# Loading the first piece of A through GpSimd's casting DMA queue, beside the first piece of B on SyncE's queue

## The chip, the cores and the metric

The kernel runs on one core of one Trainium2 chip. The metric is the device time of one execution in microseconds (us). Beside it stands a profile of one execution, whose span runs from the first instruction to the last. Engines are named as the profile names them: PE is TensorE's matmul, PEld its weight load, DVE is VectorE, ACT is ScalarE, POOL is GpSimd, SP is SyncE. SPq is SyncE's sequencer, which issues DMAs.

## What is computed

A product of two 2048x2048 fp32 matrices, then layer normalisation along each row of the product, with gamma and beta along the row.

```python
def reference(a, b, gamma, beta, eps):
    x = np.matmul(a, b)
    mean = np.mean(x, axis=-1, keepdims=True)
    var = np.var(x, axis=-1, keepdims=True)
    normalized = (x - mean) / np.sqrt(var + eps)
    return (gamma * normalized + beta).astype(np.float32)
```

## The kernel before

The product is made in fp16 with fp32 accumulation. A is cut into 16 row tiles of 128 rows, B into 16 blocks of 128 rows of the contraction (called kt), and the 2048 columns of the product into four PSUM banks of 512. B is kept whole in SBUF as fp16 (`b16`), after a cast on the chip. TensorE needs A transposed, with the contraction on the partitions; the transposed tiles are called `at`.

The row tiles fall in two kinds. Tiles 0 to 3 (the head) are worked on while B still arrives, so that a block of B that has landed is used at once for four row tiles. For this A's first 512 rows come in 16 pieces of 128 rows by 512 columns (256 KB), and B in 32 half blocks of 128 rows by 1024 columns (512 KB). Tiles 4 to 15 come later, by other helpers, with all of B in place: TensorE then only runs matmuls, one bank of 16 after the other.

A piece of the head goes through four steps, each a helper:

- `load_first(n)` (line 94): SyncE issues a DMA from HBM to an fp32 buffer `f` (pool `firstp`, 4 buffers).
- `cast_first(n)` (line 99): VectorE casts it to fp16, buffer `h` (pool `first16`, 2 buffers).
- `turn_first(n)` (line 105): TensorE transposes it in four 128x128 blocks into a PSUM bank, with `ident`, a unit matrix that GpSimd finishes on line 304.
- `keep_first(n)` (line 109): VectorE copies the bank to `at`.

A half block of B goes through `load_b` (line 76, SyncE's queue) and `cast_left` or `cast_right`, where VectorE casts 512 columns (lines 81, 86) and ScalarE the other 512 (lines 82, 87).

The order of the instructions on each engine is written out by hand: within a `manual_schedule` block every engine runs its instructions in program order. In the head the order of the DMAs on SyncE is piece 0 of A, half block 0 of B, piece 1, half block 1, and so on up to piece 3 and half block 3; the right halves follow. Loads carry one of eight completion counters in turn, so that the ninth DMA of the queue waits until the first has landed, the tenth until the second, and so on.

TensorE begins with ten matmuls on a buffer of zeros (`warm_up(10)`, line 302), whose result nobody uses; three or two more such matmuls stand in further places of the head. After the first ten comes `turn_first(0)`. Then a loop over n from 0 to 3 issues, for VectorE: `keep_first(n)`, the cast of half block n of B, `cast_first(n + 1)`; for ScalarE the other half of the cast of B; for TensorE some matmuls that are ready, the transposes of piece n + 1, and the rest of the matmuls. After the loop the four row tiles' left columns for kt 0 to 3 are completed and put by in SBUF (`put_by`, lines 150 and 152), and the right columns follow.

GpSimd has little to do in the head. Besides `ident` it issues the loads of row tiles 6 to 15 (line 115), much later, all of them plain fp32.

Of the kernel before, what the change touches and what calls it, by code (L numbers as in the profile page):

```python
# [10 lines left out]
FP16 = mybir.dt.float16  # L11
# [4 lines left out]
def kernel(  # L16
# [18 lines left out]
    nc = tc.nc  # L35
    P = 128
# [13 lines left out]
    first16 = ctx.enter_context(tc.tile_pool(name="first16", bufs=2))  # L50
# [21 lines left out]
    a_in, b_in, t_of, tile_in, part = {}, {}, {}, {}, {}  # L72

    def load_b(kt, h, queue=None):
        w = bigp.tile([P, NH], FP32, tag="big", name=f"w{kt}_{h}")
        (queue or nc.sync).dma_start(w, b_rows[kt // 4, kt % 4][:, ds(h * NH, NH)])
        b_in[kt, h] = w
# [9 lines left out]
        nc.scalar.copy(b16[:, kt, NH + NB:N], w[:, NB:NH])  # L87

    pieces = [(g, c) for c in range(4) for g in range(G)]

    def load_first(n):
        g, c = pieces[n]
        f = firstp.tile([P, 4 * P], FP32, tag="first", name=f"f{g}_{c}")
        nc.sync.dma_start(f, a[ts(g, P), ts(c, 4 * P)])
        a_in[n] = f

    def cast_first(n):
        h = first16.tile([P, P, 4], FP16, tag="h", name=f"h{n}")
        nc.vector.tensor_copy(h.rearrange("m p t -> m (p t)"), a_in[n])
        a_in[n] = h  # L100

    def turn_first(n):
        t_of[n] = psum.tile([P, 4, P], FP16, tag="c_ps", bufs=8, name=f"t_ps{n}")
        for t in range(4):
            nc.tensor.transpose(t_of[n][:, t, :], a_in[n][:, :, t], ident)
# [188 lines left out]
    with tc.manual_schedule(engines=order):  # L294
# [5 lines left out]
        def warm_up(n):  # L300
            for _ in range(n):
                nc.tensor.matmul(w_ps, warm[:, 0:P], warm, start=True, stop=True)  # L302

        nc.gpsimd.affine_select(
            out=ident, in_=ident, compare_op=AluOp.not_equal, fill=1.0,
            base=0, pattern=[[-1, P]], channel_multiplier=1,
        )
        K1 = 4
        for t in range(K1):
            load_first(t)  # L310
            load_b(t, 0)
        for t in range(K1):
            load_b(t, 1)
# [23 lines left out]


        warm_up(10)
        cast_first(0)  # L340
        turn_first(0)
        warm_up(3)
        for n in range(K1):
# [187 lines left out]
```

## Time and profile before

| | |
|---|---|
| time, median of 3 runs | 246.25 us (245.3, 246.28, 246.25) |
| the profiled execution | 244.86 us, with a span of 243.1 us |
| PE busy | 231.8 us, 95% of the span |
| DVE busy | 198.3 us, 82% |
| ACT busy | 92.9 us, 38% |
| POOL busy | 89.0 us, 37% |
| granted TensorE clock, mean | 0.994 |

When the first loads are issued and when they have landed, from the profile's list of DMA issues and its list of instructions in order of time; the landing is the issue's start plus the time to landing:

| load | name in the profile | issue | to landing | landed |
|---|---|---|---|---|
| piece 0 of A, 256 KB | f_0_106 | 0.74 | 4.4 | 5.1 |
| half block 0 of B, 512 KB | w_0_108 | 1.17 | 5.2 | 6.4 |
| piece 1 | f_0_110 | 1.64 | 5.6 | 7.2 |
| half block 1 | w_0_112 | 2.11 | 6.5 | 8.6 |
| piece 2 | f_0_114 | 2.58 | 6.7 | 9.3 |
| half block 2 | w_0_116 | 3.06 | 7.5 | 10.6 |
| piece 3 | f_0_118 | 3.71 | 7.5 | 11.2 |
| half block 3 | w_0_120 | 4.34 | 8.1 | 12.4 |

In the profile a row of the list in order of time gives the start and the length in us, the engine, the line, the operation, what it writes and reads, how many instructions are merged, and in brackets how long the engine had been idle before it and what ended that idle time. Starts are counted from the start of the span.

### The profile page before, as it was taken

Reading aid. Unit: us, or ns where it says so; the run is one execution under the profiler, and the core shown is the slowest. Engines: PE = TensorE matmul, PEld = TensorE weight load, DVE = VectorE, ACT = ScalarE, POOL = GpSimd, SP = SyncE. Lnnn points to the kernel's source line nnn. Section 1 sums busy time; section 2 is a strip of 40 time slices with the busy share of each in tenths; the row PEclk is TensorE's granted clock in tenths of the full one; section 3 lists DMA queues with packets and bytes.
Section 4 is the critical chain, followed back from the end, with each engine's and each line's share of the span. In section 5 each row is a group of like instructions: output and inputs, shape, how many; then the busy total and the mean of one; then the engine's idle time right before and its main releaser. Section 6 shows DMA issues by size and latency. Waiting matters only on the chain.

```text
span 243.1 us, 3398 instructions
## 1 busy us (share of the span) xinstructions
PE 231.8 (95%) x1139; PEld 108.2 (45%) x1139; DVE 198.3 (82%) x373; ACT 92.9 (38%) x165; POOL 89.0 (37%) x168
## 2 busy tenths in 40 slices
PE   7999899999999999999999999999999999999960
PEld 2445455444444444444444444444444444446440
DVE  1577764894399999998999899998999895966962
ACT  2373524453314330461908255370917391020020
POOL 0000000000786498897966807693760000000011
PEclk9999999999999999999999999999999999999997
DMA  4999999998699859584775626483684222030405
GB/s 163 403 402 389 369 390 412 408 409 212 187 206 302 216 164 287 180 281 124 262 204 208 229 97 235 154 291 89 215 211 175 96 86 89 32 141 0 175 0 173
DMA packets 22129, 52.66 MB, mean 217 GB/s; under 512 B 4448, under 2 KB 9056, under 8 KB 21856
## 3 DMA queue, kind: packets, MB, share of 16 engines
q1 hardware_dynamic: 16704, 41.74, 46.8%
q0 software_dynamic: 5120, 10.50, 17.3%
q10 hardware_dynamic: 288, 0.21, 0.3%
q8 instruction: 9, 0.15, 0.2%
q14 instruction: 8, 0.07, 0.1%
HBM read 35.65 MB, written 16.78 MB: 216 GB/s over the span
## 4 chain that ended last, share of the span: by engine, by line
PE 91%; DMA 3%; DVE 3%; SPq 1%; ACT 0%; issue 0%; DVEq 0%
DMA f_0_114<-in_a_dram 3%; PE ps_last_2349 L226 1%; PE ps_3_2245 L137 1%; PE ps_0_2190 L137 1%; PE ps_1_2086 L137 1%; PE ps_2_1998 L137 1%; PE ps_3_1904 L137 1%; PE ps_0_1839 L137 1%; PE ps_1_1740 L137 1%; PE ps_2_1644 L137 1%; PE ps_3_1544 L137 1%; PE ps_0_1479 L137 1%; PE ps_1_1386 L137 1%; PE ps_2_1284 L137 1%; PE ps_2_1169 L137 1%; PE ps_3_1072 L137 1%
## 5 line engine op out<-in xcount | busy, mean ns | idle before, releaser
L211 ACT ACTIVATE junk<-b_93 128x1024 f16<-128x1024 f16 x32 | 33.7, 1054 | 0.5
L115 POOL DMA_DIRECT2D p_0_240<-in_a_dram x8 | 4.5, 570 | 60.6 <-DMA p_1_211<-in_a_dram 60.6
L265 POOL TENSOR_TENSOR u_last_n<-u_last_n,gamma_b 128x128 f32<-128x128 f32 x1 | 0.5, 453 | 53.8 <-ACT u_last_n L264 53.8
L226 PEld LDWEIGHTS <-at_2062 128*128 128x128 f16 x96 | 8.8, 98 | 5.4
L137 PEld LDWEIGHTS <-at_420 128*128 128x128 f16 x64 | 6.0, 98 | 8.5 <-DVE b_93 L81 1.0
L137 PEld LDWEIGHTS <-at_1000 128*128 128x128 f16 x64 | 6.3, 98 | 7.5
L137 PEld LDWEIGHTS <-at_1240 128*128 128x128 f16 x64 | 6.3, 98 | 7.5
L137 PEld LDWEIGHTS <-at_959 128*128 128x128 f16 x64 | 6.3, 98 | 7.5
L137 PEld LDWEIGHTS <-at_1362 128*128 128x128 f16 x64 | 6.3, 98 | 7.5
L137 PEld LDWEIGHTS <-at_1716 128*128 128x128 f16 x64 | 6.3, 98 | 7.5
L137 PEld LDWEIGHTS <-at_1838 128*128 128x128 f16 x64 | 6.3, 98 | 7.5
L137 PEld LDWEIGHTS <-at_1600 128*128 128x128 f16 x64 | 6.3, 98 | 7.6
L137 PEld LDWEIGHTS <-at_1127 128*128 128x128 f16 x64 | 6.3, 98 | 7.6
L137 PEld LDWEIGHTS <-at_1009 128*128 128x128 f16 x64 | 6.2, 98 | 7.6
L137 PEld LDWEIGHTS <-at_1478 128*128 128x128 f16 x64 | 6.2, 98 | 7.6
L137 PEld LDWEIGHTS <-at_1954 128*128 128x128 f16 x64 | 6.2, 98 | 7.6
L137 PEld LDWEIGHTS <-at_421 128*128 128x128 f16 x64 | 6.1, 98 | 7.4 <-DVE at_421 L109 0.6
L137 PEld LDWEIGHTS <-at_422 128*128 128x128 f16 x64 | 6.3, 98 | 6.5
L137 PEld LDWEIGHTS <-at_423 128*128 128x128 f16 x64 | 6.3, 98 | 6.4
L302 PE MATMUL w_ps<-warm 128*128 128x512 f16 x19 | 6.5, 481 | 1.2 <-DVE warm L295 1.2
L115 POOL DMA_DIRECT2D p_0_366<-in_a_dram x8 | 4.3, 550 | 8.0 <-ACT a_0_1620 L121 5.5
L115 POOL DMA_DIRECT2D p_0_402<-in_a_dram x8 | 4.3, 549 | 5.4 <-ACT a_0_1858 L121 5.4
(575 smaller groups left out, 643.2 us busy)
## 6 DMA issues: line engine op xcount, KB each, us to landing
gamma_b<-in_gamma_dram SPq DMA_DIRECT2D x1, 1024.0 KB, 7.4
beta_b<-in_beta_dram SPq DMA_DIRECT2D x1, 1024.0 KB, 11.8
w_0_108<-in_b_dram SPq DMA_DIRECT2D x1, 512.0 KB, 5.2
w_0_112<-in_b_dram SPq DMA_DIRECT2D x1, 512.0 KB, 6.5
w_0_116<-in_b_dram SPq DMA_DIRECT2D x1, 512.0 KB, 7.5
w_0_120<-in_b_dram SPq DMA_DIRECT2D x1, 512.0 KB, 8.1
w_1_122<-in_b_dram SPq DMA_DIRECT2D x1, 512.0 KB, 8.6
w_1_124<-in_b_dram SPq DMA_DIRECT2D x1, 512.0 KB, 8.7
```

The costliest lines, as they stand in the source:

```text
L115: queue.dma_start(f[ds(32 * q, 32), c], a_pieces[q, 2 * h + c][:, ds(4 * i, 4)])
L137: nc.tensor.matmul(x_of[i, q], at[i][:, kt, :], b16[:, kt, ds(q * NB, NB)], start=(kt == lo), stop=(kt == hi - 1),)
L211: nc.scalar.activation(junk, b16[:, kt, ds(h * NH, NH)], ActFn.Copy, accum_out=b_sum[:, h, kt:kt + 1])
L226: nc.tensor.matmul(x[:, 0:w], at[last][:, t, :], b16[:, t, ds(lo, w)], start=(t == 0), stop=(t == n_kt - 1))
L265: nc.gpsimd.tensor_tensor(y, y, gamma_b[:, ds(lo, w)], AluOp.mult)
L302: nc.tensor.matmul(w_ps, warm[:, 0:P], warm, start=True, stop=True)
```

## The change

Piece 0 of A no longer goes through SyncE's queue and VectorE. A new helper lets GpSimd issue one DMA that reads the same 128 rows by 512 columns as fp32 from HBM and writes them as fp16 straight to the `h` buffer. It stands ahead of GpSimd's `affine_select`, which finishes `ident`. SyncE starts with half block 0 of B. `cast_first(0)` is gone, and the transposes of piece 0 wait for the DMA instead of VectorE. The other 15 pieces are as before.

```diff
+    def load_first_cast():
+        h = first16.tile([P, P, 4], FP16, tag="h", name="h0")
+        nc.gpsimd.dma_start(h.rearrange("m p t -> m (p t)"), a[0:P, 0:4 * P])
+        a_in[0] = h
...
+        load_first_cast()
         nc.gpsimd.affine_select(
             out=ident, in_=ident, compare_op=AluOp.not_equal, fill=1.0,
             base=0, pattern=[[-1, P]], channel_multiplier=1,
         )
         K1 = 4
         for t in range(K1):
-            load_first(t)
+            if t:
+                load_first(t)
             load_b(t, 0)
...
         warm_up(10)
-        cast_first(0)
         turn_first(0)
         warm_up(3)
```

## The prediction

> **What bounds the kernel now.** I read the page first, then the chain of waits, then the head instruction by instruction.
>
> ```profile
> span 243.1 us, 3398 instructions
> PE 231.8 (95%) x1139; PEld 108.2 (45%) x1139; DVE 198.3 (82%) x373; ACT 92.9 (38%) x165; POOL 89.0 (37%) x168
> PE   7999899999999999999999999999999999999960
> PE 91%; DMA 3%; DVE 3%; SPq 1%; ACT 0%; issue 0%; DVEq 0%
> ```
>
> PE fills every slice but the first and the last; the chain that ended last is PE for 91% and DMA for 3%. So a change in the head counts only if it moves the point from which PE runs without a gap, and then it moves the end by as much. The chain in order of time tells where that point is:
>
> ```profile
> 2.58 6.66 DMA f_0_114<-in_a_dram
> 9.24 0.03 issue
> ...
> 9.34 0.44 DVE h_465 L99
> 9.78 0.05 issue
> 9.82 0.41 PE t_ps_473 L105 x4
> 10.23 0.22 PE ps_0_467 L137
> ```
>
> The chain does not start at piece 0, which this change moves, but at piece 2 (f_0_114): it lands at 9.24, is cast, and is transposed at 9.82. From there PE goes on to 14.6, and, over some copies, to the end. Piece 0 matters only if it moves these transposes. Rows of the list in order of time, for the rounds before:
>
> ```profile
> 5.18 0.43 DVE L99 CAST h_434<-f_0_106 128x512 f16<-128x512 f32 x1 [3.96 <-DMA f_0_106<-in_a_dram]
> 5.66 0.41 PE L105 MATMUL t_ps_436<-ident,h_434 128*128 128x128 f16 x4 [0.52 <-DVE h_434 L99]
> 6.11 0.42 DVE L109 COPY at_420<-t_ps_436 128x512 f16<-128x512 f16 x1 [0.51 <-PE t_ps_436 L105]
> 7.24 0.43 DVE L99 CAST h_447<-f_0_110 128x512 f16<-128x512 f32 x1 [0.36 <-DMA f_0_110<-in_a_dram]
> 9.34 0.43 DVE L99 CAST h_465<-f_0_114 128x512 f16<-128x512 f32 x1 [0.31 <-DMA f_0_114<-in_a_dram]
> ```
>
> VectorE goes round a loop: cast a piece, wait for its transposes, keep them, cast a block of B, cast the next piece. Ahead of the casts of pieces 1 and 2 it is idle for 0.36 and 0.31 us, until the DMA: loads pace the head, with 0.67 us of slack in VectorE's loop between piece 0 and piece 2. Last, what the DMAs do (the columns after the second number are busy times by engine, then clock, DMA share, GB/s):
>
> ```profile
> 2.00:4.50 2.50, 2.50 (x7) 0.91 (x6) 0.00 (x0) 0.02 (x1) 0.00 (x0) 1.00 0.55 150
> 4.50:13.50 9.00, 8.10 (x47) 3.59 (x46) 4.80 (x12) 2.47 (x4) 0.00 (x0) 1.00 1.02 399
> ```
>
> From 4.5 us the 16 DMA engines are full, at 399 GB/s. From 2.0 to 4.5 they are busy for 55%, although SyncE has issued four loads (1.5 MB) by 2.58 us. So the ramp has room, and the rest has none.
>
> **What the Trainium skill says.** "DMA: Bandwidth & Descriptors", section "Issuing engines are not separate DMA queues": DMAs of SyncE, ScalarE and GpSimd run on the same 16 engines and interleave; a second issuer saves only issue time. The trace has one queue alone in the head, at 399 GB/s, and cannot confirm it; if it holds, moving piece 0 to another queue leaves the bytes ahead of piece 2 unchanged. Same page, "Latency and other measured facts": the first byte comes after some 0.6 us on the hardware path, 1 us on GpSimd's. The trace agrees in the order, with larger numbers: SyncE's first issue is at 0.74 and 49 GB/s are seen between 1.5 and 2.0, nothing earlier; GpSimd's first load is issued at 62.20, its queue shows no bytes before 63.6 and shows some from there, 1.4 us later. "SBUF — State Buffer", section "SBUF: two separate sides": VectorE's fast copies can keep GpSimd from writing descriptors. Here VectorE only clears three small buffers, 0.86 to 1.22 us, then sleeps until 5.18, so at most some 0.4 us. "TensorE: Matmul & The Clock Gate", Part 1: an idle window of some 3.4 us halves the clock; the trace has a gap of 0.52 us here and no drop.
>
> **The change part by part.**
>
> *VectorE:* one cast of 0.43 us goes, and 0.05 us to the transposes: 0.48 us between landing and transposing. It is worth that only if the piece lands as early as before, at 5.1. The ten warm-up matmuls end at 5.14, so the first transposes can't come before that: at most 0.52 us earlier than 5.66.
>
> *SyncE:* one issue goes from the front. Half block 0 is issued at 0.74 instead of 1.17, the later ones 0.43 to 0.47 us earlier, until landings pace them. The ninth DMA, which waits for the first, is now the tenth of before (w_1_124): it waits for half block 0, as before. Nothing starts sooner on a full DMA system, since the issues run ahead of the data anyway: piece 2 is issued 6.7 us before it lands. Worth nothing by itself. In the pool of fp32 pieces, piece 4 finds an unused buffer; the others still wait for the cast of the piece four back.
>
> *GpSimd:* one DMA is added. Its issue costs 0.55 to 0.71 us, from the rows of line 115:
>
> ```profile
> 62.20 4.50 POOL L115 DMA_DIRECT2D p_0_240<-in_a_dram  x8 [60.62 <-DMA p_1_211<-in_a_dram]
> ```
>
> eight in 4.50 us, the longest 0.714. Behind it stands only the unit matrix: from 1.28 it slips to about 1.5 and ends near 1.8, long before the transposes. GpSimd's own loads follow at 62.2 and later; their counters move by one place, onto a load long landed. No cost.
>
> *The landing of piece 0.* This is the number that decides, and no casting DMA is in the trace. Issue at 0.74, first bytes 1.4 us later: 2.1 us. From below: its 64 KB loads take 2.5 us at the shortest; 192 KB more at 399 GB/s are 0.5, so 3.7 us. From above: p_0_258's loads, beside saturated engines, took 7.9 us, so 8.6 us. Between: piece 0 and half block 0 together, 768 KB, had landed by 6.4 before. If the two queues share the engines equally, piece 0 is through when 512 KB have moved, halfway between 5.1 and 6.4: 5.75; if it gets only a third, at 6.4. I take 6.0, with transposes at 6.05: 0.39 us later than before. Half block 0 lands by 6.4 either way.
>
> *Carried forward:* the 0.39 us eat into the slack of 0.67: piece 1 is cast at 7.27 instead of 7.24, piece 2 at 9.34 as before. The break-even is a landing at 5.66 + 0.67 - 0.05 = 6.28. Piece 2's own landing stays where it is, since the bytes ahead of it are the same. PE waits 0.9 us after its warm-up instead of 0.52: far below the window above.
>
> *Sum on the span:* 243.1 + 0 = 243.1. The profiled execution, 244.86, lies 1.4 us below the median of the timed ones, which themselves span 1 us; a repeated median may move within that. I put the sum on the median, 246.25 + 0, and name 246.2.
>
> **The rivals.**
>
> *A, as above: absorbed.* 246.2 us, own range 245.3 to 247.0, chance 0.52. For it: the slack, and a chain that starts at piece 2.
>
> *B, the ramp fills: faster.* Two rings let the engines use part of the 45% of 2.5 us, 1.1 us, that they idle in the ramp. Piece 0 lands by 4.7, and the stream behind runs about 0.5 us early. The transposes of piece 0 begin at 5.14, the loop could have those of piece 2 at 5.14 + (9.82 - 5.66 - 0.67) = 8.63. Half block 3 limits next: VectorE's cast of it ends at 13.42, its first user starts at 13.96, so 0.54 without an earlier landing. Together -0.5 to -1.0; I take -0.7: 245.5 us. Against it: nothing shows that the ramp's slowness belongs to the queue rather than to the engines or HBM. Chance 0.22.
>
> *C, the casting piece is late or heavy: slower.* If converting slows the engines, the piece takes more than its 0.65 us (256 KB at 399 GB/s) of all sixteen, and everything behind is pushed. At a quarter of the rate that is 2.6 us, 1.95 more ahead of piece 2; at a half 0.65 more. A late start alone does the same to the loop: each us of landing past 6.28 is a us at the end. I take a third of the rate, +1.3: 247.5 us; it decides from 6.28 on. For it: an operation that the trace does not show, at the cold start of a queue, whose loads took 7.9 us when the engines were full. Against it: those few descriptors compete with half-idle engines. Chance 0.26.
>
> **How the numbers follow.** Outside 0.5% (1.23 us, about what a measurement of this kernel can tell from no change), B lies for about half of its chance once the runs' own spread is allowed for, 0.11, and A for 0.05 on either side; C for three quarters, 0.20. Faster 0.16, same 0.59, slower 0.25. The range takes A and most of B and C: 245.0 to 247.9.
>
> **What would show it.** A: the chain still starts at piece 2 with a landing near 9.2, and transposes of piece 0 between 5.6 and 6.3. B: a DMA share well above 0.55 from 2.0 to 4.5, piece 2 landing at 8.8 or sooner. C: the first transposes after 6.3, the chain starting at GpSimd's load, or fewer GB/s from 4.5 on. I am wrong if piece 0 lands past 6.3, or if piece 2's landing moves by more than 0.3 us.

## The result and the profile after

| | before | changed |
|---|---|---|
| time, median of 4 runs | 245.78 us | 249.11 us |
| all runs | 245.11 to 246.28 | 248.94 to 249.59 |
| ratio, with 95% interval | | 1.014, 1.0106 to 1.0175 |
| span of the profiled execution | 243.1 us | 247.2 us |
| first transposes of piece 0 / 1 / 2 / 3, us from the start of the span | 5.66 / 7.79 / 9.82 / 12.23 | 8.13 / 11.05 / 13.38 / 15.76 |

The change costs 3.3 us. Some executions of any kernel fall into a slower state; medians here and below are of all executions, while the ratios leave out two such, one of run e3 and one of run e8 below. The page of the changed kernel, with the rows that answer to those of before: PE's busy share by slices of the span, the granted clock, and the chain that ended last.

```profile
span 247.2 us, 3396 instructions
PE   7699899999999999999999999999999999999960
PEclk9799999999999999999999999999999999999995
PE 81%; DMA 8%; DVE 6%; SPq 2%; issue 1%; ACT 1%; DVEq 0%; POOLq 0%
```

PE's share of the chain went from 91% to 81%, DMA's from 3% to 8%, and the clock has a dip in its second slice. Two loads make up most of the 8%: 2.8% are piece 0, at the start, and 4.0% a half block of B much later. The chain of waits in order of time (start, length, what) shows both:

```profile
1.26 6.83 DMA h_103<-in_a_dram
8.08 0.05 issue
8.13 0.43 PE t_ps_434 L110 x4
...
10.40 0.85 PE w_ps L307 x2
11.26 0.43 PE t_ps_453 L110 x4
11.68 0.85 PE w_ps L307 x2
12.54 0.36 PE ps_0_465 L142
12.89 0.22 PE ps_1_466 L142
...
13.54 0.22 PE t_ps_471 L110 x4
...
53.63 9.78 DMA w_1_200<-in_b_dram
```

The chain no longer starts at piece 2 but at GpSimd's load: issued at 1.26, landed 6.83 us later. From 10.40 on two warm-up matmuls take 0.85 us, at 12.89 one product takes 0.22: in between PE ran at half speed. The load at 53.63 has no counterpart in the chain of the kernel before; the experiments come back to such loads. The list in order of time, and the table by stretches (after the times: PE, PEld, DVE, ACT, POOL busy, clock, DMA share, GB/s), show the same from the engines' side:

```profile
1.26 0.72 POOL L93 DMA_DIRECT2D h_103<-in_a_dram  x1 [0.81 <-POOLq L518]
8.13 0.41 PE L110 MATMUL t_ps_434<-ident,h_103 128*128 128x128 f16 x4 [2.49 <-DMA h_103<-in_a_dram]
8.58 0.42 DVE L114 COPY at_420<-t_ps_434 128x512 f16<-128x512 f16 x1 [7.36 <-PE t_ps_434 L110]
```

```profile
2.00:4.50 2.50, 2.50 (x7) 0.88 (x6) 0.00 (x0) 0.24 (x2) 0.31 (x1) 1.00 0.81 246
9.50:12.50 3.00, 3.00 (x11) 1.26 (x10) 0.95 (x4) 0.66 (x2) 0.00 (x0) 0.50 1.03 418
16.00:24.00 8.00, 7.82 (x45) 3.61 (x43) 5.49 (x13) 4.22 (x8) 0.00 (x0) 1.00 0.66 242
```

PE stood for 2.49 us, and the clock granted from 9.5 to 12.5 was 0.50. VectorE stood for 7.36 us behind the transposes of piece 0, with every later cast of the head behind it in its order. The third stretch is the surprise: from 16 to 24 us the DMAs moved 242 GB/s. In the kernel before it was

```profile
16.00:24.00 8.00, 7.82 (x46) 3.70 (x45) 6.34 (x16) 4.52 (x9) 0.00 (x0) 1.00 1.03 393
```

The waits of SyncE's queue up to 30 us say why (waited in all, times, longest). The changed kernel, then the kernel before:

```profile
SPq L99 <- DVE h_548 L104: 5.9, 1, 5.9
```

```profile
SPq L94 <- DVE h_550 L99: 2.4, 1, 2.4
...
SPq L94 <- DMA f_1_126<-in_a_dram: 1.6, 1, 1.6
```

These are waits ahead of the load of piece 8, which needs the buffer that VectorE's cast of piece 4 gives free. Before, SyncE stood 4.0 us there, 1.6 until piece 4 had landed and 2.4 more until it was cast; now it stood 5.9 us for the cast alone. The load was issued at 21.69 instead of 18.16, with the half blocks of B behind it, and the DMA engines ran dry.

### The profile page after: what moved, and what is told of

The parts are those of the page before. It is cut to its first block, busy times and chain, and to the rows that moved or that the text cites. A ratio compares the mean times of both kernels' runs of the same rounds, so it can differ in the third digit from the quotient of the medians.

```text
span 247.2 us, 3396 instructions
## 1 busy us (share of the span) xinstructions
PE 233.9 (95%) x1139; PEld 108.9 (44%) x1139; DVE 197.4 (80%) x372; ACT 92.9 (38%) x165; POOL 89.9 (36%) x169
## 4 chain that ended last, share of the span: by engine, by line
PE 81%; DMA 8%; DVE 6%; SPq 2%; issue 1%; ACT 1%; DVEq 0%; POOLq 0%
DMA w_1_200<-in_b_dram 4%; DMA h_103<-in_a_dram 3%; SPq L120 2%; PE ps_0_1008 L142 1%; PE ps_last_2347 L231 1%; PE ps_3_2243 L142 1%; PE ps_0_2188 L142 1%; PE ps_1_2084 L142 1%; PE ps_2_1996 L142 1%; PE ps_3_1902 L142 1%; PE ps_0_1837 L142 1%; PE ps_1_1738 L142 1%; PE ps_2_1642 L142 1%; PE ps_3_1542 L142 1%; PE ps_0_1477 L142 1%; PE ps_1_1384 L142 1%
## 5 line engine op out<-in xcount | busy, mean ns | idle before, releaser
L307 PE MATMUL w_ps<-warm 128*128 128x512 f16 x19 | 8.0, 563 | 1.2 <-DVE warm L300 1.2
```

## The experiments

Two questions were open after this: why GpSimd's load landed at 8.1 (its queue, or the conversion on the way), and how transposes of piece 0 that came 2.5 us late became 3.3 us at the end, and 4.1 in the profiled execution.

**Queue or conversion.** Run e1 keeps the place of the load and takes the conversion away:

```diff
-        h = first16.tile([P, P, 4], FP16, tag="h", name="h0")
-        nc.gpsimd.dma_start(h.rearrange("m p t -> m (p t)"), a[0:P, 0:4 * P])
-        a_in[0] = h
+        f = firstp.tile([P, 4 * P], FP32, tag="first", name="f0_0")
+        nc.gpsimd.dma_start(f, a[0:P, 0:4 * P])
+        a_in[0] = f
...
         warm_up(10)
+        cast_first(0)
         turn_first(0)
```

> Piece 0 on GpSimd's queue as plain fp32, cast by VectorE as before; nothing is converted in flight. Theory 'queue' (GpSimd's queue starts late and then gets its turns slowly beside SyncE's loads; converting matters little): landing 6 to 7 us after its issue, near 7.4 to 8.1 in the span, first transposes 0.5 later than that, time 249.1 to 249.8 us. Theory 'conversion' (the cast in flight is what is slow): landing by 5.8, first transposes by 6.3, time 245.8 us as before.

Measured: 249.47 us, ratio to before 1.0168 (1.0135 to 1.0201). The plain load took 6.3 us to land where the casting one took 6.8, and with VectorE's cast the first transposes came at 8.10. Its row:

```profile
f<-in_a_dram POOLq DMA_DIRECT2D x1, 256.0 KB, 6.3
```

So it is the queue; the conversion accounts for no more than the half microsecond between the two landings, with one trace of each. Run e2 is e1 with `nc.scalar.dma_start`: a second hardware queue.

> Piece 0 on ScalarE's hardware queue as plain fp32, cast by VectorE as before, beside half block 0 of B on SyncE's. Theory 'queue': a second hardware queue has no late start and an equal share, so landing 5.5 to 6.4, first transposes by 6.9, time 245.8 to 246.4 us. Rival 'beside' (any second queue loses its turns to SyncE's loads): landing 7 or later, time 247 us or more.

Measured: 245.68 us, ratio 1.0008 (0.9994 to 1.0022), no difference from before. The load was issued at 0.74, where GpSimd's was at 1.28, took 5.1 us, and the first transposes came at 6.37. Piece 0 beside half block 0 on two queues is thus harmless when the second queue is ScalarE's. Run e5 leaves the changed kernel's load alone with the engines for a while, by clearing the buffer of half block 0 twice on GpSimd, so that SyncE starts at 4.30:

```diff
         w = bigp.tile([P, NH], FP32, tag="big", name=f"w{kt}_{h}")
+        if (kt, h) == (0, 0):
+            nc.gpsimd.memset(w, 0.0)
+            nc.gpsimd.memset(w, 0.0)
```

> The changed kernel with SyncE's first load held back: its buffer is cleared twice by GpSimd after the unit matrix, so SyncE issues nothing before about 4.5 us and the casting load has the DMA engines to itself until then. Theory 'busy engines' (the queue starts late because SyncE's loads fill the engines): first bytes of GpSimd's queue 1.4 us after its issue at 1.26, by 2.9 us, and landed by 4.2 us. Theory 'cold queue' (the first load on GpSimd's queue is late whatever else runs): first bytes at 4.4 to 4.6 again, then landed by 5.5 us. The time is not the point: all loads of B come over 3 us later.

Measured: the load landed 3.5 us after its issue at 1.25, and the first transposes came at 5.41. Packets of GpSimd's queue (q0; q1 is SyncE's) in the stretches from 0 to 2.7 and 2.7 to 3.7 us of this run (queue: packets, MB, share of 16 engines):

```profile
q0 software_dynamic: 3, 0.00, 0.7%
...
q0 software_dynamic: 86, 0.08, 51.7%
```

The same for the changed kernel from 0 to 4.6 and from 4.6 to 7.9 us:

```profile
q1 hardware_dynamic: 222, 0.68, 56.1%
q0 software_dynamic: 4, 0.00, 0.5%
...
q1 hardware_dynamic: 290, 0.84, 76.9%
q0 software_dynamic: 140, 0.13, 23.1%
```

With the engines to itself the queue shows its first packets some 1.4 us after the issue, as at 62 us in the kernel before; beside SyncE's loads only after 3.3 us. Then it gets 23% of the engines' time and needs 3.2 us for what takes it 1.8 alone. Of the two theories "cold queue" falls and "busy engines" holds. The run, at 248.4 us (one execution), was no slower than the changed kernel, although all loads of B came 3.6 us later.

**What a late piece 0 costs.** Run e4 exchanges the first two loads of the kernel before on SyncE's queue:

```diff
         for t in range(K1):
-            load_first(t)
+            if t:
+                load_first(t)
             load_b(t, 0)
+            if t == 0:
+                load_first(t)
```

> The kernel before with the first two loads on SyncE exchanged: half block 0 of B ahead of piece 0 of A, nothing else. Theory 'slack' (0.67 us of slack between piece 0 and piece 2, after that each us is a us): piece 0 lands near 6.4, first transposes 6.9 instead of 5.66, 1.24 less 0.67 is 0.6 us more: 246.4 us. Rival 'no slack': 1.24 us more, 247.0 us. Rival 'piece 0 doesn't matter here': 245.8 us.

Measured: 246.98 us, ratio 1.0059 (1.0027 to 1.0092), twice what "slack" gave and near "no slack". In its profile piece 0 is transposed at 6.93 as foreseen, but piece 1 at 10.33, 2.54 later than before. PE's rows show why: it runs at half speed until then.

```profile
1.19 4.45 PE L302 MATMUL w_ps<-warm 128*128 128x512 f16 x10 [1.19 <-DVE warm L295]
...
6.93 0.61 PE L105 MATMUL t_ps<-ident,h 128*128 128x128 f16 x4 [1.30 <-DVE h L99]
7.34 1.48 PE L302 MATMUL w_ps<-warm 128*128 128x512 f16 x3
8.62 1.06 PE L137 MATMUL ps<-b,at 128*128 128x512 f16 x2
9.47 1.06 PE L302 MATMUL w_ps<-warm 128*128 128x512 f16 x2
```

Three warm-ups took 1.48 us here, 0.81 in the kernel before. This is no sign of a fallen clock: the ten warm-ups at the start had run at half speed too (4.45 us, 3.95 in the kernel before), and the clock of this trace reads 1.00 throughout. So PE hadn't come up to full speed by then, and whether the gap of 1.30 us has a part in that is not shown. The 1.23 us that e4 costs are thus not slack alone, and can't decide between "slack" and "no slack". The changed kernel's halved clock, which its trace does show, is what run e3 should take away with more warm-up:

```diff
-        warm_up(10)
+        warm_up(22)
         turn_first(0)
```

> The changed kernel with 22 warm-up matmuls at the start instead of 10, so that TensorE isn't idle for 2.5 us before piece 0 lands. Theory 'clock' (of the 3.56 us by which piece 2's transposes slipped, 2.47 are the landing and 1.1 the halved clock from 9.2 to 12.9): same landing near 8.1, no drop of the clock, time 1.1 us below the changed kernel's, 248.0 us. Rival (VectorE's loop alone sets it, the clock costs nothing): 249.1 us as before.

Measured: 248.68 us, ratio 1.0123 (1.0094 to 1.0152), with single executions from 248.02 to 251.8, too wide to tell. It was repeated (e6_long_warm) beside the changed kernel.

> The changed kernel itself once more, to stand beside the next one in the same rounds: 249.1 us.

> The changed kernel with 22 warm-up matmuls again, in more rounds, beside the changed kernel. Theory 'clock': the landing stays at 8.1 and the clock no longer drops; 0.5 to 1.1 us less than the changed kernel, 248.0 to 248.6. Rival 'VectorE's loop alone': 249.1, no difference.

Measured: the changed kernel 249.39 us, ratio 1.0157 (1.0137 to 1.0177); with 22 warm-ups 249.26, ratio 1.0173 (1.0135 to 1.0211). In the profile, of an execution of 248.37, the clock stayed at 1.00, and piece 3 was transposed at 14.62 instead of the 15.90 of the repeated changed kernel: 1.3 us won in the head, while the span fell from 246.8 to 246.6 only. The chain of waits of that run shows who took it:

```profile
25.14 0.28 ACT x L157
25.42 8.00 DMA w<-in_b_dram
33.41 0.02 issue
33.44 0.50 ACT b L82
33.94 8.22 DMA w<-in_b_dram
42.15 0.02 issue
42.18 0.44 DVE b L81
42.61 0.04 issue
42.66 2.53 PE ps L142 x11
```

A half block of B is issued when an engine gives a buffer free, lands 8 us later, is cast, frees the next: a second chain, of loads and buffers, that holds PE at 42.6. The profile of the repeated changed kernel has no load of B in its chain, and its end is 3.7 us late just as its piece 3 is. So the halved clock is real but not the whole price; the load chain is late by about as much. Whether the lateness alone starts that chain, without GpSimd's queue, is asked by e8 and e9: the kernel before with `warm_up(22)` and `warm_up(16)`, loads untouched, clock up.

> The kernel before with 22 warm-up matmuls instead of 10, so that TensorE transposes piece 0 only near 8.2 us, as in the changed kernel, while every load is issued as before and the clock stays up. Theory 'late transposes alone' (VectorE stands behind piece 0's transposes with all casts, so buffers come free late and SyncE's loads stall; the end then moves by more than 2.5 - 0.67): 248.7 to 249.3 us, and the DMA rate from 16 to 24 us falls from 393 to below 320 GB/s. Rival 'slack rule' (2.5 less 0.67, no stall of the loads): 247.6 us.

> The same with 16 warm-up matmuls: piece 0 transposed near 6.6 us, 0.9 later than before, the clock up. 'Slack rule': 0.9 less 0.67, 245.8 to 246.0 us. If the 0.67 us of slack isn't there: 246.5 us.

Measured: e8 248.84 us, ratio 1.011 (1.0074 to 1.0147), with the executions that the ratio counts from 246.61 to 249.38; e9 246.21, ratio 1.0035 (1.0021 to 1.0049). The profile of e8 is of its fastest execution, 246.61, so it doesn't show what the others lost. In it piece 0 was transposed at 7.42, not at the 8.2 foreseen, and from 16 to 24 us 336 GB/s were moved, between the 393 of before and the 242 of the changed kernel. In that of e9 piece 0 came at 6.10, 0.44 later than before, and piece 3 at 12.36, only 0.13 later. Yet its time is 0.76 us longer, and its chain again runs through loads of B, the first at 31.68:

```profile
31.23 0.35 DVE b L81
31.58 0.01 SPq L94
31.59 0.05 issue
31.64 0.02 SPq L76
31.73 0.03 issue
31.68 7.64 DMA w<-in_b_dram
```

So late transposes alone cost about 0.8 us (e9) to 2.7 us (e8, by its ratio) with the first loads issued where they were, and GpSimd's queue need not have a price of its own beyond making piece 0 late. The two rival sums for e9 both missed: the head lost 0.13 us, and by its chain the loads cost the rest. How much lateness costs how much stays open: e2, 0.71 us late at piece 0 and 0.43 at piece 3, cost nothing.

**Where the slack went.** In all these runs piece 1 followed piece 0 by 2.1 us, so VectorE's idle 0.36 us ahead of piece 1's cast didn't absorb anything. Run e11 is e2 without the two warm-ups between:

```diff
-            if n == 0:
-                warm_up(2)
             turn_first(n + 1)
```

> Piece 0 on ScalarE's queue and cast by VectorE, as in e2, and the two warm-up matmuls between the first two products and the transposes of piece 1 left out (their result is used nowhere). In e2 the transposes of piece 1 stand 2.12 us behind those of piece 0 (6.37 and 8.49), as in the kernel before (5.66 and 7.79), although VectorE's cast of piece 1 ends at 7.93. Theory 'fillers' (TensorE's own order, two products and two warm-ups, stands between, so VectorE's idle 0.36 us was no slack): piece 1 transposed 1.7 us behind piece 0, near 8.05, and piece 2 no later than 10.0 instead of 10.28; time 0.2 to 0.4 us below e2, 245.3 us. Rival 'VectorE's loop': still 2.1 us behind, no difference.

Measured: piece 1 at 8.02, 1.69 behind piece 0; piece 2 at 10.03 instead of 10.28, now again behind its own landing. The mechanism is shown, the time is not moved: 245.72 us, ratio 1.0014 (0.9999 to 1.0028). Its chain too runs through a half block of B, which lands at 39.2.

**Casting loads where they have time.** Run e7 takes the casting queue for pieces 4 to 7, which nobody needs before 17.7 us, and leaves piece 0 as before:

```diff
+    def load_cast(n):
+        g, c = pieces[n]
+        h = first16.tile([P, P, 4], FP16, tag="h", name=f"h{n}")
+        nc.gpsimd.dma_start(h.rearrange("m p t -> m (p t)"), a[ts(g, P), ts(c, 4 * P)])
+        a_in[n] = h
...
     def load_first(n):
+        if 4 <= n < 8:
+            return
...
     def cast_first(n):
+        if 4 <= n < 8:
+            return
...
+        for n in range(K1, 2 * K1):
+            load_cast(n)
+        for i in range(6, n_mt):
+            for h in (0, 1):
+                load_tile(i, h, nc.gpsimd)
         bank(*late)
```

(`first16` has four buffers, and GpSimd's later loads stand behind the new ones.)

> The kernel before, but pieces 4 to 7 of A through GpSimd's casting queue instead of piece 0 (four buffers for h instead of two, so that each load is issued once the piece four back has been transposed, from about 6 to 12.6 us). Theory 'late but hidden': beside full engines a casting load lands 5 to 8 us after its issue and is needed only from 17.7 us on; VectorE saves the cast of piece 4 ahead of 18.19 on the chain of waits, 0.35 us, and the casts of 5 to 7: 245.4 us. Rival 'converting burdens the engines' (the half blocks of B beside it land later): 246 us or more.

Measured: 244.95 us, ratio 0.9979 (0.9967 to 0.999): faster than both kernels. The loads took 6.8 us in the median, from issues at 6.54, 8.64, 10.41 and 12.79; piece 4 was transposed at 17.72 instead of 18.19, 0.47 earlier. Run e10 does the same for pieces 4 to 15, each issued after the transposes of the piece four back.

> Pieces 4 to 15 of A through GpSimd's casting queue, each issued once the piece four back has been transposed; pieces 0 to 3 as before. Theory 'late but hidden': landings 7 us after the issue, needed 8 us after it; VectorE saves twelve casts, SyncE's queue no longer waits for them: 244.9 us or some tenths less. Rival 'too late': from piece 8 on the landings come after they are needed and TensorE waits: over 246 us.

Measured: 247.15 us, ratio 1.006 (1.0042 to 1.0078). The rival was right. In e7 the casting loads had 10.8 to 12.3 us from their issue to the transposes; here TensorE came to those of pieces 9 to 15 after 5.8 to 7.2 us, and its weight load waited 0.36 to 0.57 us for each. Two of them stand in the chain:

```profile
24.39 7.35 DMA h<-in_a_dram
31.74 0.05 issue
31.78 0.43 PE t_ps L115 x4
32.21 0.28 issue
32.49 7.09 DMA h<-in_a_dram
39.59 0.05 issue
39.64 0.41 PE t_ps L115 x4
```

## Why the prediction was wrong

The forecast was 246.2 us, absorbed; the measured 249.11 lies beyond the range. Rival C had the right side and named lateness, but put its price on conversion and came out too small. By the prediction's own break-even, 6.28, a landing at 8.08 costs 1.8 us; the other 1.5 us come from the slack and from what the rule left out, below.

*The landing of piece 0* is the step that failed: 6.0 us predicted, 8.08 measured. Its terms: the issue at 0.74 came at 1.26 (0.5 us later; the profile shows no other engine that it waited for, and no run here explains it); first bytes 1.4 us after the issue came after 3.3; "the two queues share the engines equally" turned out as 23% for GpSimd. The duration of 1.4 us was read from a place at 62 us where the engines were half idle, and carried to one where SyncE had just queued 1.5 MB. The 8.6 named as the upper end held, although it is no bound: 7.9 us is the median of those loads, the longest took 9.2. A load beside busy engines should have set the value, and not only the end of a range. Why GpSimd's queue is kept out for so long, while ScalarE's (e2) is not, stays open. The section "Issuing engines are not separate DMA queues" of the Trainium skill's "DMA: Bandwidth & Descriptors" holds for e2, where the bytes just interleaved (from 3.0 to 4.5 us ScalarE's queue had 33 to 50% of the engines' time, SyncE's 53 to 59%); of GpSimd's turns it promises more than these traces show.

*The slack of 0.67 us* was mis-sized. Measured in traces whose clock did not fall: e2 is 0.71 late at piece 0 and 0.43 at piece 3, e9 0.44 and 0.13, e6_long_warm 2.67 and 2.39. So 0.28 to 0.31. VectorE's idle 0.36 ahead of piece 1 was no slack, since PE's own order (product, product, two warm-ups) ended no earlier (e11).

*"Each us of landing past 6.28 is a us at the end"* left out two things. First the clock: "PE waits 0.9 us after its warm-up instead of 0.52" was the ground for putting it at nothing, and the gap became 2.49 us. Piece 3 slipped by 3.53: 2.47 from the late piece 0, less 0.28, and some 1.3 from the halved clock. Second the loads: buffers come free late, SyncE's queue stands, and B's later half blocks set a second end. The two ends lie so close that taking one away (e6_long_warm) gains nothing that these executions can tell.

*Right were* the order and hiding of the unit matrix, half block 0 landing early (4.2 us), SyncE's earlier issues worth nothing by themselves (piece 2 landed at 9.2 in both kernels), and the test named for C: first transposes after 6.3 and a chain that starts at GpSimd's load. Rival B's premise came true without its gain: from 2.0 to 4.5 us the DMA rate rose from 150 to 246 GB/s, but in half blocks of B that nobody could use yet. Its mirror is e2, 226 GB/s there and no gain either.

*C's price* of 1.3 us assumed conversion at a third of the rate; e1 shows conversion to matter by at most 0.5 us. Being late is what cost, as C's sentence on a late start said in passing.

## What to carry to other kernels

Take the latency of a DMA queue from a place in the trace that is as busy as the place it is moved to: here 1.4 us to the first bytes became 3.3 beside a full queue. A casting load on GpSimd's queue relieved VectorE well where its data had some 11 us until it was needed (e7), not where TensorE came to it after 5.8 to 7.2 us (e10), and not at the first piece that everything stands behind. An idle gap of an engine is slack only if nothing else, like another engine's own order, fills the same stretch; and a delay at the head is to be followed through the buffers it holds as well as along the engine that bounds.

## What the runs showed of the hardware that was not expected

- GpSimd's queue beside SyncE's loads: landings 6.2 to 7.5 us after the issue (e1, e7, e10 and the changed kernel), 3.5 us with the engines free (e5). ScalarE's hardware queue in the same place took 5.1 us (e2).
- The clock of TensorE fell to 0.50 for 3.4 us in four traces, in or after idle gaps of 1.96 us (e5), 2.49 and 2.56 (the changed kernel twice) and 3.20 (e1). After 0.92 us (e6_long_warm) it did not. In the changed kernel it fell at 9.3, over 1 us after PE had gone back to work at 8.13. "TensorE: Matmul & The Clock Gate", Part 1, of the Trainium skill puts the fall at an idle window of some 3.4 us; shorter gaps were enough here.
- The clock in the profile is not PE's speed from the start. It reads 1.00 during the ten warm-ups of the changed kernel, of e2 and of e4, which took 4.45 us, some 0.43 each, where later ones took 0.22.
- The ramp: with half block 0 first, 226 to 271 GB/s from 2.0 to 4.5 us (e2, e4), with piece 0 first 150. It was worth nothing here, as the pieces of A are what the head waits for.
